# A chunk's triangular inverse, multiplied into b and into the output matrix before the chain

## The chip, the cores and the metric

The kernel runs on one core of a Trainium2 chip, in one launch. The metric is device time in microseconds, the median of several runs. The engines are named as in the profile: PE (TensorE, matmuls into PSUM banks), DVE (VectorE), ACT (ScalarE), POOL (GpSimd) and SP (SyncE, which issues every DMA). Work between engines is ordered by semaphores; each engine takes its own instructions in order.

## The reference: what is computed

One layer of a hybrid decoder, for a prompt of 1024 tokens and for 8 sample sequences of one token each, width 1024, all in fp32. A projection of 1024 x 9360 feeds two branches, a gated linear attention (GLA, 4 heads) and RWKV-7 (16 heads of 64); each branch is projected up, gated, merged, projected out and normed. The change is in RWKV-7 on the prompt, whose recurrence is, per head and token:

```python
def step(S, inp):
    rt, wt, kt, vt, kkt, at = inp
    sa = jnp.einsum('bhvk,bhk->bhv', S, -kkt)
    S = S * wt[:, :, None, :] + sa[..., None] * (kkt * at)[:, :, None, :] + vt[..., None] * kt[:, :, None, :]
    y = jnp.einsum('bhvk,bhk->bhv', S, rt)
    return S, y
```

Over a chunk of 64 tokens this can be written with matrices. With a, z, b and k the rows of the chunk scaled by their decays, the vectors sa solve a unit lower triangular system, whose matrix is built from a and b; the state at the chunk's end is the decayed sum of the old state, b times sa and k times v; and the outputs are z times the old state plus an output matrix (built from z, b and k) times sa and v. The inverse of the triangular system is known before the state is.

## The kernel before

**Tiling.** The tokens are done in two passes of 512 (the first takes the 8 samples along). The projection runs row by row: 128 output columns against 512 tokens in 24 matmuls a bank (8 blocks of the depth, three products each of high and low halves), in the first pass in two parts of 256 and 264 columns, into the PSUM banks `proj`. These are the matmuls `proj<-xs,wpart` of the profile; they make up most of PE's time and fill the gaps of everything else. Two RWKV heads are one pair, so there are 8 pairs in each pass and 16 in all, and each pair has 8 chunks of 64 tokens.

**Order.** The kernel is written as streams (generators that yield one instruction at a time). A planner, `Order.run`, picks at each step the stream whose next instruction can start first by its own cost table, with a priority by kind (`PRIO`, `ON_PE`), and so fixes every engine's order at build time. All instructions are therefore recorded on one line, L217, and are told apart by tiles. Buffers are handed out by tag (`get`, `free`). PSUM has 2 banks `proj`, 4 `big`, 1 `pch` and 1 `pY`. An engine called `self.C` lets the planner choose ACT or DVE, `self.E` DVE or POOL.

**A pair** goes through five stages.

- `front` makes the scaled rows: a and z in `az`, b and k in `bk`. PE multiplies them (`big<-az,bk`), and DVE masks the products into `gg`: per chunk the system's matrix (k index 0) and the output matrix (k index 1), for both heads. The diagonal 32x32 blocks of all systems go through DRAM (`LD`) into a layout with one block per partition, and DVE solves them in 31 steps, each one multiply (`Xt<-X,wide`) and one add (`X<-X,Xt`). The inverted blocks go through DRAM (`XD`) into the buffer `XT`, and into `X2`. There are two buffers `XT` of 128 x 1024.
- `back` makes the off-diagonal block of each 64x64 inverse: four transposes on DVE put blocks from `XT` in `X1`; four products on 128*32 tiles (`big<-X,L`), one copy to `A`, four products (`big<-X,A`), four copies into `XT`.
- `turn` transposes b and k (`big<-cons,bk`, the result `bt` again in the buffer `bk`) and v (into `u`, a buffer `wide`).
- `chain` goes through the chunks one after the other. Each has three products of 128x128 in the bank `pch`: the right-hand side (`pch<-wide,gg`), copied by DVE to a buffer `rh`; the inverse times it (`pch<-rh,XT`), copied as two 64x64 halves into `u` by ACT or DVE; and the state (`pch<-wide,bk`), from which DVE makes the next chunk's state. A chain starts when the chain of the pair before it has ended. At its end up to 16 products of 64x64 (z times the states, `pY<-row,az` and `big<-row,az`) and 16 of 128x64 (the output matrix times `u`, `pY<-wide,gg` and `big<-wide,gg`) make the outputs of the pair.
- `norm` norms and gates the outputs and stores them.

Each fp32 product stands in the trace as two matmul records.

Of the kernel before, what the change touches and what calls it, by code (L numbers as in the profile page):

```python
# [20 lines left out]
P = 128  # L21
# [11 lines left out]
C = 64  # L33
# [15 lines left out]
    "Xt": ([P, P], 1), "L1": ([P, P], 1), "A": ([P, P], 1), "S": ([P, GDV], 2), "Sp": ([P, C], 2), "s0p": ([P, C], 2), "rh": ([P, P], 2),  # L49
# [373 lines left out]
class Kern(Order):  # L423
# [711 lines left out]
    def front(self, c, p, st, d):  # L1135
# [95 lines left out]
        XT = (yield from self.get("XT")).rearrange("p (c h t) -> p c h t", c=NCH, h=2)  # L1231
# [21 lines left out]
        d.AZ, d.BK, d.G, d.XT, d.v, d.bonus, d.pc, d.L, d.L1, d.X2 = AZ, BK, GG, XT, st[2], st[1], pc, L_, L1, X2  # L1253

    def back(self, d):
        GG, XT = d.G, d.XT

        H = NCH // 2
        X1 = (yield from self.get("X1")).rearrange("p (x t) -> p x t", t=P)
        q = [slice(32 * n, 32 * n + 32) for n in range(4)]  # L1260
        for h in range(2):
            for n in range(2):
                g = 2 * h + n
                yield self.V.transpose(X1[q[g], :, q[g]], XT[q[2 * h], H * n:H * n + H, h, 0:32])
        pA = yield from self.bank("big", [P, P])
# [574 lines left out]
```

## Time and profile before

| | |
|---|---|
| median of 3 runs | 1489.15 us (1487.49, 1489.15, 1490.96) |
| profiled execution, its own time | 1487.92 us |
| its span, first to last instruction | 1486.1 us |
| busy PE, DVE, ACT, POOL | 1449.8, 1194.8, 857.7, 113.6 us |
| mean granted clock of PE | 0.996 |
| DMA | 318.96 MB, 66.8% of the 16 engines' span on the main queue |

A line of the groups reads: line, engine, operation, output tile <- input tiles, the array's rows*columns (PE), shape, count, then busy us and mean ns of one, then the engine's idle time just before them and what ended it. The timeline has start, duration, engine and count of merged neighbours. A line of a tile's view has the shortest, median and longest duration in ns and the first and last start in us.

### The profile page before, as it was taken

What the parts mean: (1) busy time and instruction counts of PE and PEld (TensorE: products, weight loads), DVE (VectorE), ACT (ScalarE), POOL (GpSimd) and SP (SyncE); (2) the same over time, 40 slices, a digit from 0 to 9 for tenths busy, and PEclk for the clock granted to TensorE, in tenths of its full rate; (3) what the DMA queues carried; (4) which work ended last, traced back from release to release, by engine and by line L of the source; (5) the groups of instructions that cost most, each with busy time, mean ns of one, the idle gap of its engine ahead of it and who ended that gap; (6) DMA issues with size and microseconds to landing.
All of it is one profiled execution on the core that took longest, in us unless ns stands there. A gap on an engine that the chain in (4) does not pass through costs nothing. (4 is left out here: it accounts for less than half of the span.)

```text
span 1486.1 us, 31563 instructions
## 1 busy us (share of the span) xinstructions
PE 1449.8 (98%) x11158; PEld 1260.4 (85%) x11158; DVE 1194.8 (80%) x3255; ACT 857.7 (58%) x2196; POOL 113.6 (8%) x208
## 2 busy tenths in 40 slices
PE   9999999999999999999999999999999999999997
PEld 6998999899989998787777777878787898988786
DVE  6697889888998899879878989898877866755665
ACT  5666776676767776665754555474547645544210
POOL 1001010201010102000101020111001000000000
PEclk9999999999999999999999999999999999999999
DMA  8886786678676877566566556656564766888432
GB/s 299 273 285 202 250 296 214 226 253 295 202 258 211 294 229 258 170 224 188 160 198 179 155 190 191 192 154 188 174 189 138 229 210 221 295 293 271 139 107 85
DMA packets 211258, 318.96 MB, mean 215 GB/s; under 512 B 91811, under 2 KB 107180, under 8 KB 211100
## 3 DMA queue, kind: packets, MB, share of 16 engines
q1 hardware_dynamic: 211100, 316.93, 66.8%
q8 instruction: 89, 1.46, 0.4%
q14 instruction: 69, 0.57, 0.1%
HBM read 197.19 MB, written 118.61 MB: 212 GB/s over the span
## 5 line engine op out<-in xcount | busy, mean ns | idle before, releaser
L217 PE MATMUL proj<-xs,wpart 128*128 128x264 f32 (+2 forms) x5640 | 1017.7, 327 | 1.4 <-DVE row L217 0.8
L217 PEld LDWEIGHTS proj<-xs,wpart 128*128 128x128 f32 x5640 | 808.5, 189 | 80.3 <-issue 9.9
L217 ACT CAST wpart<-wraw 128x512 fp32r<-128x512 f32 x210 | 130.2, 623 | 103.5 <-PE proj L217 49.6
L217 DVE TENSOR_TENSOR row<-row 128x512 f32<-128x512 f32 (+7 forms) x321 | 166.3, 524 | 12.4 <-ACT row L217 5.6
L217 DVE TENSOR_TENSOR wpart<-wraw,wpart 128x512 fp32r<-128x512 f32 x207 | 145.2, 702 | 32.3 <-ACT wpart L217 31.4
L217 ACT ACTIVATE row<-row 128x512 f32<-128x512 f32 (+5 forms) x213 | 128.8, 610 | 14.4 <-DMA row<-sg 6.5
L217 POOL TENSOR_TENSOR row<-row 128x512 f32<-128x512 f32 (+5 forms) x64 | 72.7, 1143 | 746.3 <-DVE row L217 396.4
L217 DVE TENSOR_TENSOR Xt<-X,wide 128x60 f32<-128x60 f32 (+24 forms) x496 | 104.8, 211 | 11.7 <-DMA wide<-LD 1.8
L217 DVE TENSOR_TENSOR X<-X,Xt 128x60 f32<-128x60 f32 (+24 forms) x496 | 105.4, 213 | 10.0
L217 ACT ACTIVATE row<-proj,omu 128x256 f32<-128x256 f32 (+1 forms) x99 | 54.0, 546 | 93.5 <-PE proj L217 93.3
L217 PE MATMUL big<-xs,wpart 128*128 128x256 f32 (+2 forms) x576 | 101.7, 332 | 0.0
L217 PEld LDWEIGHTS big<-xs,wpart 128*128 128x128 f32 x576 | 87.7, 194 | 9.7 <-issue 0.2
L217 DVE SCALAR_TENSOR_TENSOR wide<-pch,pc,s0p 64x64 f32<-64x64 f32 x208 | 58.7, 282 | 32.9 <-PE pch L217 28.0
L217 ACT COPY row<-wide 64x64 f32<-64x64 f32 x240 | 57.9, 241 | 40.2 <-DVE wide L217 34.7
L401 ACT ACT_TABLE_LOAD x62 | 79.5, 1283 | 1.1
L217 DVE SCALAR_TENSOR_TENSOR row<-proj,pv,row 128x255 f32<-128x255 f32 (+1 forms) x99 | 56.3, 569 | 22.4 <-ACT tail L217 13.7
L217 PE MATMUL big<-row 128*32 128x32 f32 (+4 forms) x936 | 65.3, 241 | 1.4 <-ACT row L217 1.4
L217 ACT COPY row<-big 128x128 f32<-128x128 f32 (+6 forms) x134 | 38.7, 318 | 42.2 <-PE big L217 36.7
L217 ACT COPY wide<-pch 64x64 f32<-64x64 f32 x159 | 32.8, 206 | 47.0 <-PE pch L217 45.1
L217 ACT ACTIVATE row<-proj 128x128 f32<-128x128 f32 (+4 forms) x136 | 36.9, 324 | 37.4 <-PE proj L217 37.0
L217 PE MATMUL pch<-wide,gg 128*128 128x128 f32 x256 | 51.6, 283 | 5.5 <-DVE wide L217 4.7
L217 PEld LDWEIGHTS pch<-wide,gg 128*128 128x128 f32 x256 | 42.3, 189 | 16.1 <-PE proj L217 4.7
(249 smaller groups left out, 1992.6 us busy)
## 6 DMA issues: line engine op xcount, KB each, us to landing
w<-wpart SPq DMA_DIRECT2D x146, 512.0 KB
wpart<-w SPq DMA_DIRECT2D x146, 512.0 KB
wraw<-w_in SPq DMA_DIRECT2D x146, 256.0 KB
wide<-LD SPq DMA_DIRECT2D x64, 128.0 KB
wraw<-w_up_gla SPq DMA_DIRECT2D x32, 256.0 KB
wraw<-w_up_rwkv SPq DMA_DIRECT2D x32, 256.0 KB
sg<-row SPq DMA_DIRECT2D x16, 260.0 KB
row<-sg SPq DMA_DIRECT2D x16, 260.0 KB
```

The lines of the kernel that those rows point to most:

```text
L217: ways.append((eng, lambda call=call: call(out, *args, **kw), price(eng, name, out, args, ins)))
L401: self.nc.scalar.preload_act_table_set(self.table)
```

## The change

The system is now solved the other way round: DVE goes through the columns from the last to the first, so that `X` becomes the inverse itself and not its transpose. Each step's multiply reads a column of `L` (`LT`, a view with 32 elements between neighbours) where it read a row; the 31 steps have the same sizes in the opposite order. The inverse of a chunk is kept per head without the zeros between the heads, as `XI`, in half of an `XT` buffer.

In `back`, `X1` is loaded from DRAM and `X2` is computed: the four products `big<-X,L` come first, four copies write `X2`, eight transposes of 32x64 write `A`, and the four products `big<-X,A` and four copies follow as before.

`turn` gets a new last step. For each chunk, each head and each of b (`bt`) and the output matrix (`gg`, k index 1), a 64x64 product with `XI`: 32 products, in two `big` banks, and eight copies of 64x256 which put the results back in place of b and of the output matrix.

In `chain` the product with `XT`, the copy to `rh` and the buffers `rh` are gone: the right-hand side itself is copied into `u`, as two 64x64 halves, and the state's product and the outputs use the multiplied b and output matrix.

The core of the diff:

```diff
@@ front
-        for j in range(31):
-            w, ni = 31 - j, j // 4 + 1
-            tv = tm[:, :ni * w].rearrange("p (s t) -> p s t", t=w)
-            yield V.tensor_mul(tv, X[:, 0:ni, j:j + 1].to_broadcast([P, ni, w]),
-                               L[:, j:j + 1, j + 1:].to_broadcast([P, ni, w]))
-            yield V.tensor_add(X[:, 0:ni, j + 1:], X[:, 0:ni, j + 1:], tv)
+        LT = L.rearrange("p s t -> p t s")
+        for j in range(31, 0, -1):
+            i, ni = j // 4, 8 - j // 4
+            tv = tm[:, :ni * j].rearrange("p (s t) -> p s t", t=j)
+            yield V.tensor_mul(tv, X[:, i:, j:j + 1].to_broadcast([P, ni, j]),
+                               LT[:, j:j + 1, :j].to_broadcast([P, ni, j]))
+            yield V.tensor_add(X[:, i:, :j], X[:, i:, :j], tv)
...
-        X2 = (yield from self.get("X2")).rearrange("p (g t) -> p g t", t=P)
+        X1 = (yield from self.get("X1")).rearrange("p (x t) -> p x t", t=P)
...
+        for h in range(2):
+            for n in range(2):
+                b, o = slice(64 * h + 32 * n, 64 * h + 32 * n + 32), h * NCH + H * n
+                yield self.S.dma_start(X1[b, :, b], XD[o:o + H].rearrange("c s t -> s c t"))
...
-                yield self.S.dma_start(XT[HS[h]][b, :, h, b], XD[n * NCH:(n + 1) * NCH].rearrange("c s t -> s c t"))
-
-        for x in range(H):
-            b = slice(32 * x, 32 * x + 32)
-            yield self.S.dma_start(X2[b, :, b], XD[2 * NCH + x::H].rearrange("g s t -> s g t"))
+                yield self.S.dma_start(XI[HS[h]][b, :, b], XD[n * NCH:(n + 1) * NCH].rearrange("c s t -> s c t"))
@@ back
-                yield self.V.transpose(X1[q[g], :, q[g]], XT[q[2 * h], H * n:H * n + H, h, 0:32])
...
-        yield self.C.copy(A_, pA)
+        for x in range(H):
+            for h in range(2):
+                yield self.V.transpose(A_[q[x], 2 * h:2 * h + 2], XI[q[2 * h + 1], x::H, 32:64])
+        for x in range(H):
+            yield self.C.copy(X2[q[x], :, x], pA[q[x]].rearrange("p (g t) -> p g t", t=32))
...
-                yield self.C.copy(XT[q[2 * h], H * n:H * n + H, h, 32:64], pZ[q[2 * h + n]])
+                yield self.C.copy(XI[q[2 * h + 1], H * n:H * n + H, 0:32], pZ[q[2 * h + n]])
@@ turn
+        pf = yield from self.get("big", 2)
+        pf = [y.rearrange("p (x k t) -> p x k t", k=2, t=C) for y in pf]
+        yield together([self.P.matmul(pf[h][HS[x % 2], x // 2, k], d.XI[hs, x], (bt[hs, x, h], d.G[hs, x, 1, h])[k], start=True, stop=True)
+                        for i in range(0, NCH, 2) for k in range(2) for x in (i, i + 1) for h, hs in enumerate(HS)], 0.5)
+        for k in range(2):
+            for h, hs in enumerate(HS):
+                for n in range(2):
+                    yield self.C.copy(d.G[hs, n::2, 1, h] if k else bt[hs, n::2, h], pf[h][HS[n], :, k])
+        self.free(*pf, d.XI)
@@ chain
             yield self.P.matmul(pr, GG[:, x, 0], u, start=True, stop=True)
-            rh = yield from self.get("rh")
-            yield V.tensor_copy(rh, pr)
-            self.free(pr)
...
-            pu = yield from self.bank("pch", [P, 2, C])
-            yield self.P.matmul(pu, XT[:, x], rh, start=True, stop=True)
-            self.free(rh)
             for h, hs in enumerate(HS):
-                yield self.C.copy(u[hs, h], pu[hs, h])
-            self.free(pu)
+                yield self.C.copy(u[hs, h], pr[hs, h])
+            self.free(pr)
```

The planner makes a new order of the whole program from it. PE, in the chain of the second pass's sixth pair, before (`proj` rows are projection matmuls, `big<-part,headsr` and `big<-az,bk` belong to the next pair's front):

```order
L217 MATMUL pch<-wide,gg 128x128
L217 MATMUL proj<-xs,wpart 128x512 x6
L217 MATMUL pch<-rh,XT_168 128x128
L217 MATMUL proj<-xs,wpart 128x512 x5
L217 MATMUL pch<-wide,bk 128x128
L217 MATMUL proj<-xs,wpart 128x512 x3
L217 MATMUL big<-part,headsr 128x512
L217 MATMUL proj<-xs,wpart 128x512
L217 MATMUL pch<-wide,gg 128x128
```

and the chunks of the same pair with the change:

```order
L217 MATMUL pch<-wide,bk 128x128
L217 MATMUL proj<-xs,wpart 128x512 x7
L217 MATMUL pch<-wide,gg 128x128
L217 MATMUL proj<-xs,wpart 128x512 x5
L217 MATMUL pch<-wide,bk 128x128
L217 MATMUL proj<-xs,wpart 128x512 x5
L217 MATMUL pch<-wide,gg 128x128
L217 MATMUL proj<-xs,wpart 128x512 x5
L217 MATMUL pch<-wide,bk 128x128
```

The middle product of a chunk is gone, and the projections between two products stay five to seven. Over the whole program the products `pch<-rh,XT` go from 128 to 0.

PE again, in the turn of that pair, with the change (before, only the transposes `big<-cons,bk` and `big<-cons,row` and 32 projections stood between the inverse and the chain):

```order
L217 MATMUL big<-X_173,A 32x128 x4
L217 MATMUL proj<-xs,wpart 128x512 x5
L217 MATMUL big<-cons,bk 128x64 x16
L217 MATMUL proj<-xs,wpart 128x512 x2
L217 MATMUL big<-cons,row 128x128 x4
L217 MATMUL proj<-xs,wpart 128x512 x5
L217 MATMUL big<-bk,XT_168 64x64 x4
L217 MATMUL big<-gg,XT_168 64x64 x4
L217 MATMUL big<-bk,XT_168 64x64 x4
L217 MATMUL big<-gg,XT_168 64x64 x4
```

The four groups of 64x64 products come twice (32 products, the last 16 follow), after everything that they read has been given some projections' time. Over the program the order has 512 of them.

DVE, in the same pair with the change, from the inverse to the first chunks of the chain:

```order
L217 STREAM_TRANSPOSE A<-XT_168 32x64 x8
L217 TENSOR_REDUCE row<-row 128x8
L217 BN_STATS st<-row 128x6
L217 BN_AGGR st<-st 128x2
L217 SCALAR_TENSOR_TENSOR row<-row,nkk 128x512
L217 COPY XT_168<-big 32x4x32 x4
```

Eight transposes stand where four of 32x128 stood. Of the 128 new copies of 64x256 over the program, the order has 49 on DVE and 79 on ACT; of the 256 copies of 64x64 in the chains, 159 on DVE and 97 on ACT, which were 97 and 159; of the 64 copies to `X2`, 5 on DVE and 59 on ACT, for 16 to `A`. DMA issues stay 1331.

More of the change, by code (lines that the diff above doesn't have):

```diff
@@ L1261, in back @@
         for h in range(2):
             for n in range(2):
-                g = 2 * h + n
-                yield self.V.transpose(X1[q[g], :, q[g]], XT[q[2 * h], H * n:H * n + H, h, 0:32])
-        pA = yield from self.bank("big", [P, P])
-        yield together([self.P.matmul(pA[q[x]], d.L1[:, x], X1[:, x], start=True, stop=True) for x in range(H)])
-        A_ = yield from self.get("A")
-        yield self.C.copy(A_, pA)
-        self.free(pA, X1, d.L1)
-        pZ = yield from self.bank("big", [P, H, 32])
@@ L1271, in back @@
-        yield together([self.P.matmul(pZ[q[g]], A_[:, q[g]], d.X2[:, g], start=True, stop=True) for g in range(4)])
-        for h in range(2):
-            for n in range(2):
-                yield self.C.copy(XT[q[2 * h], H * n:H * n + H, h, 32:64], pZ[q[2 * h + n]])
+                yield self.C.copy(XI[q[2 * h + 1], H * n:H * n + H, 0:32], pZ[q[2 * h + n]])
         for h, hs in enumerate(HS):
             yield self.C.copy(GG[hs, :, 0, h], d.AZ[hs, :, 0])
-        self.free(pZ, A_, d.X2)
+        self.free(pZ, A_, X2)
@@ L1353, in chain @@
         self.free(*pY, ss_)
-        self.free(AZ, BK, u_, GG, XT, pc)
+        self.free(AZ, BK, u_, GG, pc)
         if c.i:
```

24 lines of the change are left out of this document (15 added, 9 removed).

## The prediction

> **What bounds the kernel now.** The page first: the engines' busy shares and the slices of the span.
>
> ```profile
> span 1486.1 us, 31563 instructions
> ...
> PE 1449.8 (98%) x11158; PEld 1260.4 (85%) x11158; DVE 1194.8 (80%) x3255; ACT 857.7 (58%) x2196; POOL 113.6 (8%) x208
> ...
> PE   9999999999999999999999999999999999999997
> ...
> PEclk9999999999999999999999999999999999999999
> ```
>
> TensorE (PE) has work in every slice, at the full granted clock, and lacks only 36.3 us of the span (1486.1 - 1449.8). But matmuls overlap, so a row's busy time is no price: what one product costs the stream has to be read from start to start in the timeline. Before that, the groups of PE that the change touches (busy us, mean ns of one record, idle before it and who ended it):
>
> ```profile
> L217 PE MATMUL pch<-rh,XT 128*128 128x128 f32 x256 | 51.1, 281 | 4.1 <-DVE rh L217 4.1
> L217 PE MATMUL pch<-wide,bk 128*128 128x128 f32 x256 | 50.5, 279 | 2.0 <-DVE wide L217 1.3 <-ACT wide L217 0.7
> L217 PE MATMUL big<-X,A 128*32 128x128 f32 x128 | 7.0, 284 | 2.9 <-DVE row L217 1.3 <-DMA X<-XD 1.2 <-DVE A L217 0.3
> L217 PE MATMUL big<-X,L 128*32 128x128 f32 x128 | 6.8, 285 | 1.7 <-DVE X L217 1.7
> ```
>
> The first is the product that goes. An fp32 product stands as two records, so its 256 records are 128 products, eight in each of 16 pairs. Next, the timeline of a chain, PE alone (start, us, form, count):
>
> ```profile
> 139.76 1.33 PE L217 MATMUL proj<-xs,wpart 128*128 128x256 f32 x9
> 140.93 0.38 PE L217 MATMUL pch<-rh,XT 128*128 128x128 f32 x2
> 141.07 1.35 PE L217 MATMUL proj<-xs,wpart 128*128 128x264 f32 x9
> 142.25 0.38 PE L217 MATMUL pch<-wide,bk 128*128 128x128 f32 x2
> 142.39 1.45 PE L217 MATMUL proj<-xs,wpart 128*128 128x264 f32 x10
> 143.69 0.38 PE L217 MATMUL pch<-wide,gg 128*128 128x128 f32 x2
> 143.82 0.36 PE L217 MATMUL proj<-xs,wpart 128*128 128x256 f32 x1
> ```
>
> The chain's latency is not the bound. Between two of its products PE does 9 or 10 projection matmuls, and the last product of this kind starts long before the end of the span:
>
> ```profile
> L217 PE MATMUL pch<-rh,XT x256: 270/273/421, 136.7 to 1260.4; 128*128 128x128 f32 x128
> ```
>
> So a shorter chain gives nothing by itself. What counts is PE's own work, and PE's waits.
>
> **What leaves PE.** The chain of waits shows projections with nothing between them, 48 of 256 or 264 columns and 48 of 512:
>
> ```profile
> 1187.40 5.79 PE proj L217 x48
> ...
> 1315.04 11.11 PE proj L217 x48
> ```
>
> One takes 0.1206 us, or 0.2315 us. From 139.76 to 143.82 are 4.06 us with 28 projections (28 x 0.1206 = 3.38) and three products: (4.06 - 3.38)/3 = 0.228 us for each, half of the busy time that its group shows. 128 products leave: **-29.2 us**.
>
> **What comes to PE.** Per pair, 32 products of 64x64 by 64 columns, four different quadrants of the array in turn: 64 records, 512 products in all. The trace has the same form in the same order of quadrants, in the outputs' state part (16 products, 32 records):
>
> ```profile
> 894.24 0.95 PE L217 MATMUL proj<-xs,wpart 128*128 128x512 f32 x3
> 895.11 0.27 PE L217 MATMUL pY<-row,az 64*64 64x64 f32 x1
> ...
> 895.22 0.22 PE L217 MATMUL pY<-row,az 64*64 64x64 f32 x1
> ...
> 895.57 0.22 PE L217 MATMUL pY<-row,az 64*64 64x64 f32 x1
> ...
> 895.59 0.22 PE L217 MATMUL big<-row,az 64*64 64x64 f32 x1
> 895.74 0.69 PE L217 MATMUL pY<-wide,gg 128*64 128x64 f32 x16
> 896.25 0.64 PE L217 MATMUL big<-wide,gg 128*64 128x64 f32 x16
> 896.82 0.96 PE L217 MATMUL proj<-xs,wpart 128*128 128x512 f32 x3
> ```
>
> From 895.22 to 895.57 six groups of four records start, 0.058 us a group. The 32 records with the way out of the form take 895.11 to 895.74, 0.63 us; 32 more are eight groups, 0.46 us: 1.09 us. Going in, three projections and the change of form took 0.87 us where three take 0.69: up to 0.18 us. Coming back to projections, the second 16 records took 0.57 us against 0.51 for the first: 0.06 us. So a pair pays 1.09 to 1.33 us. I take 1.29 (the full entry may hold a little of what stands ahead of it): 16 x 1.29 = **+20.6 us**, ends 17.4 and 21.3. The products on 128*32 tiles keep their number.
>
> The Trainium skill says in "TensorE: Matmul & The Clock Gate", section "Wait — 56ns, not 53.3ns?", that start to start never drops below about 25 ns however small a matmul is; by that, an estimate, the 64 records would take 1.6 us and the 16 pairs some 29 us, and the change would give nothing on PE. The rows speak against it here: 0.058 us for four is 14.5 ns.
>
> **Waits.** The copy to rh goes with its 4.1 us of idle PE: -4.1. The product with bk now stands behind two copies of 64x64, as before, but the order puts 159 of these 256 on DVE instead of 97, and DVE is the engine that was late; it may inherit from nothing to the whole 4.1: I take +2, the middle, since its row shows 2.0 now with the smaller DVE share. The new block waits for the inverse (copies out of the big banks), and the first chunk for eight more copies; behind the block on PE stand projections, so all of PE waits with it, and its two big banks are held from the other streams till the copies are done. The nearest rows are the X products: (2.9 + 1.7) us on 32 blocks, 0.14 us a block; 16 new ones: +2.3, from 0 (the order puts projections and transposes ahead of them) to 16 x 0.53 us at which the whole gain is gone, a rival below.
>
> **What DVE and ACT get.**
>
> ```profile
> L217 DVE COPY rh<-pch 128x128 f32<-128x128 f32 x128 | 37.0, 289 | 17.5 <-PE pch L217 14.7
> L217 DVE COPY wide<-pch 64x64 f32<-64x64 f32 x97 | 21.4, 221 | 13.7 <-PE pch L217 11.3 <-issue 0.3
> L217 DVE STREAM_TRANSPOSE X<-XT 32x128 f32<-32x128 f32 x64 | 19.2, 300 | 4.9 <-DMA XT<-XD 4.3
> L217 DVE COPY wide<-big 64x256 f32<-64x256 f32 x31 | 13.1, 423 | 4.7 <-PE big L217 4.2
> ...
> L217 ACT COPY wide<-pch 64x64 f32<-64x64 f32 x159 | 32.8, 206 | 47.0 <-PE pch L217 45.1 <-DVE wide L217 0.3
> L217 ACT COPY wide<-big 64x256 f32<-64x256 f32 x33 | 12.1, 367 | 6.0 <-DVE wide L217 5.5
> L217 ACT COPY XT<-big 32x128 f32<-32x128 f32 x43 | 11.0, 256 | 7.3 <-PE big L217 6.7
> ```
>
> The order gives DVE 49 of the new 64x256 copies (49 x 0.423 = 20.7), 62 more chain copies (13.7) and 128 transposes of 32x64 for 64 of 32x128 (0.15 to 0.30 each; at 0.235 it is 30.1 - 19.2 = 10.9), and takes 128 rh copies (-37.0) and nine other 64x256 copies (-3.8): about +4.5 us. ACT gets 79 of the 64x256 copies (29.0) and 59 of 32x128 (15.1), less 62 chain copies (-12.8): about +31 us on an engine idle for 42% of the span. That cover hides both; without it, the eight copies at a hand-over (some 3 us on one engine) would keep projection banks full. The transfers stay as many and as large: four of 16 KB to X1 instead of four to X2, four of 32 KB to XI.
>
> The solve reads L down its columns, 128 bytes from element to element, in 31 multiplies a pair with 1560 elements in all. The trace has no long read of that kind. The nearest rows: the first product of a GLA head, whose writes jump (128x512, 128 elements apart), a plain 128x512, and two short ones, of which the last reads X with 128 bytes between its eight elements:
>
> ```profile
> 222.64 1.10 DVE L217 TENSOR_TENSOR row<-row 128x512 f32<-128x512 f32 x1
> ...
> 115.03 0.69 DVE L217 TENSOR_TENSOR row<-row 128x512 f32<-128x512 f32 x1
> ...
> 107.10 0.17 DVE L217 TENSOR_TENSOR Xt<-X,wide 128x16 f32<-128x16 f32 x1
> ...
> 108.51 0.16 DVE L217 TENSOR_TENSOR Xt<-X,wide 128x8 f32<-128x8 f32 x1
> ```
>
> The jumping write cost 0.41 us on 512 elements, 0.80 ns each; the jumping read of eight shows nothing. So 0 to 1560 x 0.80 ns = 1.25 us a pair on DVE; I take 0, by the row that also reads.
>
> **Sum**: -29.2 + 20.6 - 4.1 + 2.0 + 2.3 = -8.4 us. The profiled execution took 1487.92 us, its span and 1.8 us around it, so 1479.5. It lies 1.2 us under the median of the three runs, so the median should come to 1489.15 - 8.4, rounded **1481**.
>
> **Rivals.**
>
> *The gain comes back as waits* (no change, 1486 to 1492). The chain's three products a chunk become two, but both stand behind DVE. 256 products that wait 8.4/256 = 0.033 us longer eat it all; now rh and bk wait 6.1 us on 256 products, 0.024. For it: DVE at 80%, and a new order of everything. Against: DVE gets only 4.5 us more, and the order keeps five or more long projections between the chain's products. Chance 0.22.
>
> *The column read of L is slow and the inverse comes late* (slower). At 1.25 us a pair, unknown to the planner, PE stands at the X products and the new block; if every pair pays it, 16 x 1.25 = 20 us, 1481 + 20 = 1501. It is slower from (8.4 + 3)/16 = 0.71 us a pair. For it: the jumping write, and the 1.7 us that PE once waited for X. Against: the short read, and that the order has other work between solve and use. Chance 0.12. The Trainium skill speaks for this one: in "SBUF — State Buffer", section "Specifications (TRN2)", the row on cachelines says that full bandwidth needs two hits or more in a 16-byte line and that each step to a new line pays a penalty. The write agrees; no run here shows a long read.
>
> *The 64x64 block is dearer than its twin*, say as its 128x64 neighbours: 0.51 us for 16 records, 2.05 for 64, with 0.24 for the changes 2.29 us a pair, 36.6 us: -8.4 + 16.0 = +7.6, 1497. Against: same form, same order of quadrants, two banks in turn. Chance 0.09.
>
> That the change doesn't shorten the chain is out: the order shows two pch products a chunk.
>
> **How the numbers follow.** The forecast (PE's work falls) has 0.57. Its own range is 1470 (no new waits, the block at its low end, a few us by the new order) to 1486. The rivals have 0.22, 0.12 and 0.09. Range 1470 to 1496: it leaves out most of the late inverse and a little below. About 0.2%, 3 us, is what a measurement of this kernel can tell from no change. Faster by more 0.57; within it 0.24 (the second case and a mild form of the dear block); slower 0.19.
>
> **What the changed profile would show.** No rh group; pch products only with gg and bk; PE idle before the bk product near 4 us and not above 8. 512 products of 64x64 in 16 blocks of 1.2 to 1.4 us each: 2 us would be the dear block. Xt<-X,wide at the old duration for its size, for its largest form as here (with 0.80 ns on each of 76 elements it would be 305 ns):
>
> ```profile
> L217 DVE TENSOR_TENSOR Xt<-X,wide 128x76 f32<-128x76 f32 x16 | 3.9, 244 | 0.3
> ```
>
>  PE's busy time down by some 7 us, its idle time within 3 us of 36. I am wrong if PE's idle time grows by 8 or more, or if the new order leaves projections so late that the last chain's products start well after 1260.

## The result and the profile after

The changed kernel takes **1497.41 us** (median of 6 runs, 1493.07 to 1499.2); the kernel before took 1488.32 us beside it. The ratio is **1.0058, 95% interval 1.0038 to 1.0079**: slower by some 9 us, where 1481 was forecast, and above the range, which ended at 1496. The profiled execution took 1497.11 us, its span 1495.3. From the page of the changed kernel:

```profile
span 1495.3 us, 33318 instructions
PE 1445.9 (97%) x11926; PEld 1249.3 (84%) x11926; DVE 1210.3 (81%) x3249; ACT 882.2 (59%) x2283; POOL 136.1 (9%) x235
PE   9999999999989999999979999999999999999997
```

PE's busy time fell, 1449.8 to 1445.9, but its idle time grew from 36.3 to 49.4 us (1495.3 - 1445.9), 13.1 where the prediction had put its limit at 8. Two slices that were full are not full any more. The groups of the changed kernel by shape (busy us, mean ns | idle before, and what ended it):

```profile
L217 PE MATMUL pch<-wide,gg 128*128 128x128 f32 x256 | 51.7, 283 | 6.5 <-DVE wide L217 6.1 <-DMA wide<-Sp 0.2
L217 PE MATMUL pch<-wide,bk 128*128 128x128 f32 x256 | 51.7, 283 | 0.9 <-DVE wide L217 0.7
L217 DVE STREAM_TRANSPOSE A<-XT 32x64 f32<-32x64 f32 x128 | 30.3, 237 | 8.0 <-DMA XT<-XD 5.9
L217 PE MATMUL big<-part,headsr 128*128 128x512 f32 x64 | 27.6, 442 | 9.0 <-DVE Xt L217 7.7 <-DVE part L217 1.0 <-ACT bk L217 0.3
L217 PE MATMUL big<-bk,XT 64*64 64x64 f32 x512 | 16.8, 224 | 0.0
L217 PE MATMUL big<-gg,XT 64*64 64x64 f32 x512 | 16.0, 218 | 0.0
L217 PE MATMUL big<-X,A 128*32 128x128 f32 x128 | 7.1, 284 | 2.5 <-DVE A L217 1.4 <-ACT X L217 1.1
L217 PE MATMUL big<-X,L 128*32 128x128 f32 x128 | 6.8, 282 | 8.2 <-DMA XT<-XD 4.4 <-DMA X<-XD 2.4 <-DVE row L217 1.0
L217 DVE TENSOR_TENSOR Xt<-X,wide 128x76 f32<-128x76 f32 x16 | 4.7, 293 | 0.3
```

and two groups of the kernel before that the prediction does not show:

```profile
L217 PE MATMUL pch<-wide,gg 128*128 128x128 f32 x256 | 51.6, 283 | 5.5 <-DVE wide L217 4.7 <-ACT wide L217 0.3
...
L217 PE MATMUL big<-part,headsr 128*128 128x512 f32 x64 | 27.2, 430 | 3.8 <-DVE part L217 3.0 <-ACT part L217 0.7
```

The reader is to see three things. The chain's products wait less than before (6.5 + 0.9 us for 5.5 + 4.1 + 2.0), and the new block never waits. The first product of the inverse, `big<-X,L`, waits 8.2 us for 1.7, and 6.8 of the 8.2 ended with transfers out of `XD`; the second, `big<-X,A`, waits 2.5 us for 2.9. The multiplies of the solve take longer: 293 ns for the largest, 244 before.

The new block itself, in the timeline of PE in the changed kernel (start, us, form, count):

```profile
1078.87 1.40 PE L217 MATMUL proj<-xs,wpart 128*128 128x512 f32 x5
1080.21 0.34 PE L217 MATMUL big<-bk,XT 64*64 64x64 f32 x8
1080.37 0.30 PE L217 MATMUL big<-gg,XT 64*64 64x64 f32 x8
...
1081.07 0.30 PE L217 MATMUL big<-gg,XT 64*64 64x64 f32 x8
1081.30 1.19 PE L217 MATMUL proj<-xs,wpart 128*128 128x512 f32 x4
```

Five projections before it are 5 x 0.2315 = 1.16 us, to 1080.03; the next projections start at 1081.30. The block costs 1.27 us; 1.29 was forecast.

The longest wait of the changed kernel stands in the slice that shows 7. Its timeline, the rows that matter for it:

```profile
762.63 5.26 PE L217 MATMUL proj<-xs,wpart 128*128 128x512 f32 x22
...
763.69 2.33 POOL L217 TENSOR_TENSOR row<-row 128x512 f32<-128x512 f32 x1 [9.21 <-ACT row L217]
...
774.97 0.43 DVE L217 CAST part<-row 128x512 fp32r<-128x512 f32 x1
...
775.54 1.43 PE L217 MATMUL big<-part,headsr 128*128 128x512 f32 x2 [7.66 <-DVE Xt L217]
```

and two stretches of it, with the busy time of each engine and the granted clock:

```profile
core 0: us, PE busy (x) PEld busy (x) DVE busy (x) ACT busy (x) POOL busy (x), PEclk, DMA share, GB/s
...
765.00:772.00 7.00, 2.89 (x13) 2.03 (x11) 6.79 (x25) 4.73 (x10) 1.03 (x1) 1.00 0.50 152
772.70:779.50 6.80, 3.96 (x20) 2.95 (x21) 6.11 (x19) 1.04 (x2) 0.62 (x1) 0.50 0.07 12
```

In the planner's order this product follows a run of projections, and its `part` is there only at 775.40. Until then DVE, 6.79 of 7.00 us busy, works through two things at once: the solve of one pair and the rows that `big<-part,headsr` of the next needs. (The view names the multiply `Xt`, whose end lay nearest.) From 772.67, still in the wait, to 779.50 PE is granted half its clock. So a wait is followed by a loss of its own. To count this, I call *work* PE's busy time less half of its busy time at the half clock, the start-up included, and *idle* its gaps over 0.1 us up to the end of its last matmul, with the 1.7 us ahead of the first. The kernel before has work 1442.3 and idle 28.0, the changed kernel 1437.5 and 41.2; busy at half the clock before the end are 6.3 and 13.8 us. At the start PE is busy for 8.8 and 2.9 us before the full clock is granted; in the kernel before, projections start 0.22 us apart until then and 0.12 us after it. How long this lasts differs from execution to execution (full clock comes at 4.6 to 10.9 us in the twenty traces), so its share is no effect of the change. The 9.2 us of longer span are: work -4.8, idle with the ends +13.1, half clock +3.7, start-up -2.9.

### The profile page after: what moved, and what is told of

Read it like the earlier page. It is cut to its first block, busy times and chain, and to the rows that moved or that the text cites. A ratio compares the mean times of both kernels' runs of the same rounds, so it can differ in the third digit from the quotient of the medians.

```text
span 1495.3 us, 33318 instructions
## 1 busy us (share of the span) xinstructions
PE 1445.9 (97%) x11926; PEld 1249.3 (84%) x11926; DVE 1210.3 (81%) x3249; ACT 882.2 (59%) x2283; POOL 136.1 (9%) x235
## 4 chain that ended last, share of the span: by engine, by line
PE 40%; DVE 15%; DMA 6%; issue 4%; SPq 4%; ACT 3%; POOL 0%; POOLq 0%; DVEq 0%; ACTq 0%
PE proj L217 18%; PE big L217 17%; DVE row L217 5%; SPq L217 4%; PE pY L217 3%; DVE Xt L217 2%; DVE X L217 2%; PE pch L217 2%; ACT row L217 2%; DVE wide L217 1%; DMA wide<-LD 1%; DMA row<-xT 1%; DVE pair L217 1%; DVE wpart L217 1%; DMA XT<-XD 1%
## 5 line engine op out<-in xcount | busy, mean ns | idle before, releaser
L217 PE MATMUL proj<-xs,wpart 128*128 128x256 f32 (+2 forms) x5640 | 1008.2, 327 | 1.5 <-DVE row L217 0.8
L217 DVE TENSOR_TENSOR row<-row 128x256 f32<-128x256 f32 (+8 forms) x313 | 164.1, 530 | 7.3 <-ACT row L217 2.4
L217 DVE TENSOR_TENSOR wpart<-wraw,wpart 128x512 fp32r<-128x512 f32 x202 | 140.5, 698 | 32.2 <-ACT wpart L217 29.7
L217 POOL TENSOR_TENSOR row<-row 128x256 f32<-128x256 f32 (+4 forms) x72 | 78.1, 1090 | 642.1 <-ACT row L217 263.2
L217 DVE TENSOR_TENSOR Xt<-X,wide 128x60 f32<-128x60 f32 (+24 forms) x496 | 125.3, 253 | 13.0 <-DMA wide<-LD 1.7
L217 PE MATMUL big<-xs,wpart 128*128 128x512 f32 (+2 forms) x552 | 95.7, 328 | 1.7 <-ACT xs L217 1.3
L217 PEld LDWEIGHTS big<-xs,wpart 128*128 128x128 f32 x552 | 82.4, 191 | 11.2 <-ACT xs L217 1.5
L217 ACT CAST xs<-row 128x520 fp32r<-128x520 f32 (+1 forms) x64 | 38.5, 623 | 32.6 <-PE pY L217 9.8
L217 PEld LDWEIGHTS pch<-wide,bk 128*128 128x128 f32 x256 | 42.8, 189 | 12.6 <-issue 3.4
```

Source lines behind the costliest of these rows:

```text
L217: ways.append((eng, lambda call=call: call(out, *args, **kw), price(eng, name, out, args, ins)))
```

## The experiments

All runs stand beside the kernel before, whose median was 1487 to 1489 us each time. Labels are given as names. A trace is one execution, up to 4.5 us from the median of its kernel.

### The column read

**e1_row_read** is the changed kernel with a row of L read instead of the column. What it reads is zeros, so the inverse is the identity; the planner sees the same sizes, and the order on every engine is that of the changed kernel. **e2_before_col** is the reverse, the kernel before with the column read.

```diff
# e1_row_read, in the changed kernel
-                               LT[:, j:j + 1, :j].to_broadcast([P, ni, j]))
+                               L[:, j:j + 1, :j].to_broadcast([P, ni, j]))
# e2_before_col, in the kernel before
+        LT = L.rearrange("p s t -> p t s")
-                               L[:, j:j + 1, j + 1:].to_broadcast([P, ni, w]))
+                               LT[:, j:j + 1, j + 1:].to_broadcast([P, ni, w]))
```

> The changed kernel with one edit: each of the 31 multiplies of the solve reads a row of L where it read a column (it reads wrong numbers, so the inverse comes out as the identity). Every engine's order stays the same, instruction for instruction. Theory A (the column read costs 0.80 ns an element, 42 ns on the mean multiply, 20 us of DVE in all, and the late inverse and what DVE does behind it hold PE up): the multiplies fall from 253 to about 211 ns, the three PE waits of 7.7, 2.6 and 2.5 us go or shrink below 1 us, the clock has no more dips than before, and the time is that of the forecast, 1478 to 1484 us. Theory B (the waits come from the new order and from the new copies, and would stand with any multiply): 1494 us or more, with the long waits at the same places.

> The kernel before with one edit: the multiplies of its solve read a column of L where they read a row (wrong numbers, the inverse comes out as the identity), in the same order on every engine. Theory A: multiplies at 253 instead of 211 ns, 20 us more on DVE, and PE waits as in the changed kernel: 8 us or more, 1496 or later. Theory B: the old order has the slack for it, and the time stays within 3 us of 1488.

Measured: e1_row_read 1487.99 us (ratio to before 1.0008, 0.9993 to 1.0023), e2_before_col 1493.43 (1.0047, 1.0028 to 1.0065). The largest multiply, first in e1_row_read, then in e2_before_col:

```profile
L217 DVE TENSOR_TENSOR Xt<-X,wide 128x76 f32<-128x76 f32 x16 | 3.7, 234 | 0.3
```

```profile
L217 DVE TENSOR_TENSOR Xt<-X,wide 128x76 f32<-128x76 f32 x16 | 4.9, 307 | 0.3
```

Each order has its own pair: 234 ns with the row and 293 with the column in the order of the change, 244 and 307 in the order of before, 0.8 ns for each of 76 elements. All 496 multiplies of the changed order take 105.4 us with the row and 125.3 with the column, 1.25 us a pair. This is the upper bound of the prediction. In time it is worth 9.4 us in the changed order (1497.4 - 1488.0; 8.1 if each is counted against the kernel before that ran beside it) and 6.5 us in the order of before; a third pair of one order, below, gives 12.8. The wrong numbers are not what costs: the identity comes with the row in e1_row_read and with the column in e2_before_col, and the column is the slower in both. But with the row read the changed kernel is level with the one before, not at the 1478 to 1484 us of theory A, and its waits are still there. From e1_row_read:

```profile
L217 PE MATMUL big<-part,headsr 128*128 128x512 f32 x64 | 27.3, 433 | 8.7 <-DVE Xt L217 7.4 <-DVE part L217 1.3
L217 PE MATMUL big<-X,A 128*32 128x128 f32 x128 | 7.1, 284 | 1.3 <-DVE A L217 1.3
L217 PE MATMUL big<-X,L 128*32 128x128 f32 x128 | 6.8, 282 | 6.5 <-DMA XT<-XD 2.3 <-DMA X<-XD 1.8 <-ACT row L217 1.0
```

PE waits 7.4 us at the place of the 7.7, and 6.5 us for the first products. The slow read does not explain the missing 8 us of gain.

**e3_told** tells the planner of the slow read; **e4_act_copy** lets ScalarE write a transposed copy of L once a pair, so that DVE reads rows of it.

```diff
# e3_told, in the planner's price of a multiply
+        if name == "tensor_mul" and any(int(list(x.ap)[-1][0]) == 32 for x in ins):
+            return 0.068 + n / 960 + 0.0008 * n
# e4_act_copy
...
-        LT = L.rearrange("p s t -> p t s")
+        LT_ = yield from self.get("LT")
+        LT = LT_.rearrange("p (t s) -> p t s", s=32)
+        yield A.copy(LT, L.rearrange("p s t -> p t s"))
```

> The changed kernel, whose planner is told 0.8 ns an element more for the multiplies with the column read; the multiplies themselves stay slow. The planner makes another order. Theory A, if lateness against the plan is what costs: PE waits fall to the 28 us of before and the time to 1480 to 1487; if it is DVE's load itself that costs, 1490 to 1497. Theory B: any order may be lucky or not, 1485 to 1500, and the multiplies have no part in it.

> The changed kernel with L transposed once per pair by a copy on ACT (128 x 1024, some 1 to 2 us, on an engine 40% idle) into a buffer of its own, so that the multiplies read rows with the right numbers. Theory A: multiplies at 211 ns, time 1479 to 1486, a little above the run with the row read, since the copy stands in the pair's way for 1 to 2 us. Theory B: as the changed kernel, 1492 to 1500.

Measured: e3_told 1491.51 us (1.0031, 1.0015 to 1.0047), e4_act_copy 1507.33 (1.0139, 1.0117 to 1.0161). e3_told decides nothing: its time lies in the ranges of both theories, and PE's idle time, by the count above, is 36.3 us. e4_act_copy is slower than either of its theories allowed. The groups of e4_act_copy show why the copy is no cure:

```profile
L217 ACT COPY LT<-wide 128x1024 f32<-128x1024 f32 x16 | 33.4, 2086 | 3.2 <-DMA wide<-LD 3.1
...
L217 DVE TENSOR_TENSOR Xt<-X,LT 128x60 f32<-128x60 f32 (+24 forms) x496 | 107.6, 217 | 21.2 <-ACT LT L217 11.2
```

The multiplies are short again (217 ns in the mean), but the copy takes 2.09 us and stands ahead of the solve, where DVE sits idle for 11.2 us in all until it ends: more than the 1.25 us that it saves, on the path of every pair. The order is a new one too, so how much of the 10 us over the changed kernel is the copy's is open.

**e5_lay**, a complete kernel, stores X with the columns outer and the eight blocks inner, so that an element of L's column is read several times in a row; ScalarE brings the result back into rows.

```diff
-        X = X_.rearrange("p (i t) -> p i t", t=32)
+        X = X_.rearrange("p (t i) -> p t i", i=8)
...
+            tv = tm[:, :ni * j].rearrange("p (t s) -> p t s", s=ni)
+            yield V.tensor_mul(tv, X[:, j:j + 1, i:].to_broadcast([P, j, ni]),
+                               L[:, :j, j:j + 1].to_broadcast([P, j, ni]))
...
+        Y_ = yield from self.get("XY")
+        yield A.copy(Y_.rearrange("p (i t) -> p i t", t=32), X.rearrange("p t i -> p i t"))
```

> The changed kernel, complete, with the substitution's X stored columns outer and its 8 blocks innermost, so that L's column is read with each element repeated in the inner loop and not by a jump to the next; ScalarE copies X back into rows once per pair. Slow-read theory: the multiplies Xt go back from 253 ns to about 210 to 225 ns and the time falls to 1486 to 1491 us, near the row-read kernel's 1488.0. Rival (the order that comes out decides, whatever the read costs): the added copy shifts the order, and the time lies anywhere in 1470 to 1497 with the long PE waits deciding; the multiplies are short all the same.

Measured: 1494.04 us (1.0048, 1.0036 to 1.006). The multiplies are as short as expected, the time is 3 us above the range of the slow-read theory:

```profile
L217 ACT COPY XY<-X 128x256 f32<-128x256 f32 x16 | 11.3, 708 | 13.3 <-DVE X L217 13.2
...
L217 DVE TENSOR_TENSOR Xt<-X,wide 128x60 f32<-128x60 f32 (+24 forms) x496 | 110.5, 223 | 17.0 <-DMA wide<-LD 6.5
```

So a shorter solve alone is not enough. The copy adds 0.7 us to each pair's path, and the order is new; which of the two took the gain back is not separated here.

### Other orders of the same kernels

The planner fixes one order for each kernel. To see how much of a difference is the luck of that order, one of its numbers was changed slightly: `SPARE` (time it leaves for an operand of PE) from 0.4 to 0.42 (names with n1), or its hop price for products from 0.2 to 0.21 (n2).

```diff
# n1_before, n1_row, n1_after, e5_lay_n1
-SPARE = 0.4
+SPARE = 0.42
# n2_before, n2_row, e5_lay_n2
-HOP = {"P": 0.2, "D": 0.26, "G": 0.14, "V": 0.14, "A": 0.14}
+HOP = {"P": 0.21, "D": 0.26, "G": 0.14, "V": 0.14, "A": 0.14}
```

> The kernel before, with one constant of the planner moved by 0.02 us (SPARE 0.40 to 0.42, what it keeps free ahead of a PE instruction that waits for another engine): the same instructions in another order. Theory C (the old order was a lucky one; a new order of either program costs PE about 10 us in waits and clock): 1493 to 1502. Theory D (orders hardly differ, and the long waits come from what the change itself adds): within 4 us of 1487.

> The changed kernel with the row read (inverse wrong, as the identity) and SPARE 0.42: the changed instructions in another order, with fast multiplies. Theory C: the long waits of 7.4, 2.5 and 2.4 us are this order's own and lie elsewhere or not at all; time anywhere from 1478 to 1495, and on the mean of the orders some 8 us below the kernel before in the same two nudged orders. Theory D: waits of the same size at the same stages, 1486 to 1490.

> The kernel before, with another constant moved by 0.01 us (what the planner allows from PE to the engine that reads its bank, 0.20 to 0.21). Theory C: 1493 to 1502. Theory D: within 4 us of 1487.

> The changed kernel with the row read (inverse wrong, as the identity) and the second constant moved. Theory C: from 1478 to 1495, some 8 us below the kernel before with the same constant on the mean of the two. Theory D: 1486 to 1490, the 7 us wait of the headsr product at the start of the second pass stands again.

> The changed kernel, its column read kept, with SPARE 0.42. Slow-read theory: 1472 to 1477 us, 6 to 10 us above the row-read kernel at the same value (1466.3), since the column read cost 6.5 us in the order of before and 9.4 us in the changed order; TensorE's work, half-clock loss and waits taken apart, 7 us below that of the kernel before at this value. Rival (the slow read is hidden wherever no long wait lies): 1466 to 1469 us, as the row read.

> The same new layout with the planner's SPARE at 0.42 in place of 0.4, the value at which the row-read kernel took 1466.3 and the kernel before 1475.5. Slow-read theory with order as a second term: 1466 to 1476 us, below the kernel before at the same value. Rival (order alone): no relation to the other kernels at this value, 1470 to 1497 us.

> The same new layout with the planner's hop price for products at 0.21 in place of 0.2, where the row-read kernel took 1490.0 and the kernel before 1479.0. If the three nudges say anything of the layout itself, 1486 to 1491 us again; if order decides, anywhere in 1466 to 1497 us.

Measured, with the ratio to the kernel before: n1_before 1475.5 (0.9925, 0.9905 to 0.9946), n1_row 1466.29 (0.9867, 0.9848 to 0.9886), n2_before 1479.0 (0.9943, 0.9922 to 0.9964), n2_row 1490.03 (1.003, 1.0015 to 1.0044), n1_after 1479.08 (0.9946, 0.9931 to 0.9962), e5_lay_n1 1499.26 (1.0085, 1.0072 to 1.0098), e5_lay_n2 1491.76 (1.0028, 1.0016 to 1.004).

One and the same computation lies anywhere in a band of 11 us (before) to 24 us (row read), by nothing but the order, and with it the engine that takes an operation which may run on two. The theories missed this: n1_before and n2_before were to take 1493 to 1502 us or to stay within 4 us of 1487, and n1_row came 12 us below its lowest range. The order of the kernel before was the worst of its three, so a new order was no neutral thing. n1_row and n1_after have one order and differ in the read alone: 12.8 us. The expectation for n1_after was 1472 to 1477, and it came 2 us above; the rival, that the read is hidden (1466 to 1469), is out. That the new layout would follow the row read to 1466 to 1476 us with `SPARE` 0.42 was wrong by more than 20 us: a value of the planner's numbers doesn't carry its luck from one kernel to the next.

### The fold and the inverse apart

What was still open: which part makes the waits that the row read left. **fold_0** is the kernel before with the fold alone: the block, its copies and the chain of two products, but the inverse made in the old way (its transpose goes into the block, so the outputs are not the reference's). **inv_0** is e1_row_read without the fold: the new way to the inverse, and the old chain. The names with 1 and 2 have the planner's two values above.

```diff
# fold_0, in the kernel before: turn and chain as in the change, with
+        yield together([self.P.matmul(pf[h][HS[x % 2], x // 2, k], d.XT[hs, x, h], (bt[hs, x, h], d.G[hs, x, 1, h])[k], start=True, stop=True)
...
# inv_0, in e1_row_read: front and back as in the change, with
+        XT = (yield from self.get("XT")).rearrange("p (c h t) -> p c h t", c=NCH, h=2)
...
+            yield self.P.matmul(pu, XT[:, x], rh, start=True, stop=True)
```

> The kernel before with the fold alone: the 64x64 block and its 8 copies stand behind the turn, the chain takes two products, and the inverse is made as before (row read, X1 by transposes; its transpose goes into the block, so the numbers are wrong). TensorE's work should be about 7 us below before's 1442.8 in any case. Theory F (the fold itself, with its shorter chain, makes the waits): idle time between the first and the last matmul 33 us or more, with waits over 2 us, and 1484 to 1492 us. Theory I (the new making of the inverse makes them): idle 20 to 28 us, no wait over 2 us, 1474 to 1480 us. Theory C (each new order draws its own waits): neither holds at every value of the planner's numbers.

> The fold alone with SPARE 0.42, where the kernel before took 1475.5 us with 20 us of idle and the row-read changed kernel 1466.3 with as much. Theory F: idle over 28 us, 1476 us or more. Theory I: idle near 20 us, 1466 to 1470 us. Theory C: no relation.

> The fold alone with the hop price for products at 0.21, where the kernel before took 1479.0 us. Measured so far: the fold alone 1467.5 us in the first order and 1482.7 with SPARE 0.42, the inverse alone 1497.0 and 1484.4. Theory I (the new making of the inverse makes the waits): 1467 to 1477 us, below before at this value, with TensorE's work 7 us lower. Theory C (luck of each order): anywhere in 1465 to 1492 us.

> The changed kernel without the fold: the new making of the inverse (row read, X1 by transfers, A by transposes, so the inverse is the identity as in the row-read run), and before's chain with three products a chunk and the rh copy. TensorE's work as before, about 1443 us. Theory F: idle 20 to 28 us, no wait over 2 us, 1476 to 1487 us. Theory I: first products waiting for the transfers of XD 3 to 7 us in all and waits over 2 us, idle 33 us or more, 1488 to 1496 us. Theory C: neither at every value.

> The new making of the inverse without the fold, SPARE 0.42. Theory F: as the kernel before at this value, 1475 us with idle near 20 us. Theory I: 1480 us or more, with the waits for XD's transfers and a wait over 2 us. Theory C: no relation.

> The new making of the inverse without the fold, hop price 0.21. Theory I: slower than the kernel before at this value (1479.0), as in the other two orders (by 9 to 10 us): 1484 to 1496 us, with waits of the first products for XD's transfers. Theory C: anywhere in 1470 to 1497 us.

Measured: fold_0 1467.53 (0.9863, 0.9846 to 0.9879), fold_1 1482.73 (0.9974, 0.9962 to 0.9987), fold_2 1485.19 (0.9983, 0.9967 to 0.9999); inv_0 1496.98 (1.0068, 1.0053 to 1.0083), inv_1 1484.43 (0.9982, 0.9973 to 0.9992), inv_2 1483.67 (0.9966, 0.9951 to 0.998). All kinds in three orders (first, `SPARE` 0.42, hop 0.21); the last three columns are from the traces, in us: PE's work (mean), PE's waits for the transfers out of `XD`, and the time from the end of the solve to the second products `big<-X,A` (median over 16 pairs):

| kind | times | mean | work | idle | waits for XD | solve to second products |
|---|---|---|---|---|---|---|
| before | 1487.0, 1475.5, 1479.0 | 1480.5 | 1441.8 | 28.0, 20.0, 19.3 | 1.2, 0, 0.6 | 14.4, 14.6, 14.2 |
| fold alone | 1467.5, 1482.7, 1485.2 | 1478.5 | 1433.5 | 21.6, 31.3, 33.3 | 0.5, 0.2, 0 | 14.3, 14.6, 14.2 |
| inverse alone | 1497.0, 1484.4, 1483.7 | 1488.4 | 1441.7 | 32.6, 28.5, 26.1 | 5.7, 6.4, 7.7 | 17.4, 17.9, 17.1 |
| both, row read | 1488.0, 1466.3, 1490.0 | 1481.4 | 1434.2 | 33.2, 19.7, 35.6 | 4.1, 2.9, 5.1 | 17.2, 17.3, 17.0 |
| both, column read (the change) | 1497.4, 1479.1 | 1488.2 | 1437.4 | 41.2, 28.7 | 6.8, 4.0 | 17.2, 17.5 |
| both, X with columns outer (e5) | 1494.0, 1499.3, 1491.8 | 1495.0 | 1435.5 | 37.9, 45.2, 38.6 | 5.7, 19.3, 11.7 | 17.9, 18.8, 18.9 |

The columns say different things. *Work*: the fold takes 8.3 us out of PE (1439.9 to 1443.3 us in the three orders of before, 1433.1 to 1434.3 with it), and the inverse's new making nothing that shows (1438.5 to 1445.1). *Waits for XD* and *solve to second products* hang on the inverse alone, with no exception in twelve row-read orders: 0 to 1.2 us of waits and 14.2 to 14.6 us with the old making, 2.9 to 7.7 us and 17.0 to 17.9 with the new one. All waits of the two kinds of products `big<-X` together are 1.7 to 4.6 us with the old making and 5.1 to 12.1 with the new. What makes the path longer is seen in one pair. The kernel before, timeline:

```profile
905.25 0.18 DVE L217 TENSOR_TENSOR X<-X,Xt 128x8 f32<-128x8 f32 x1
905.49 2.58 SPq L217 DMA_DIRECT2D XD<-X  x4
911.43 1.85 SPq L217 DMA_DIRECT2D XT<-XD  x4
...
916.51 1.24 DVE L217 STREAM_TRANSPOSE X<-XT 32x128 f32<-32x128 f32 x4
...
918.17 0.43 PE L217 MATMUL big<-X,L 128*32 128x128 f32 x8
919.09 0.25 ACT L217 COPY A<-big 128x128 f32<-128x128 f32 x1
...
919.89 0.43 PE L217 MATMUL big<-X,A 128*32 128x128 f32 x8
```

and inv_0, the same pair:

```profile
905.16 0.17 DVE L217 TENSOR_TENSOR X<-X,Xt 128x8 f32<-128x8 f32 x1
905.39 2.57 SPq L217 DMA_DIRECT2D XD<-X  x4
911.32 1.79 SPq L217 DMA_DIRECT2D X<-XD  x4
913.15 1.91 SPq L217 DMA_DIRECT2D XT<-XD  x4
...
915.73 0.43 PE L217 MATMUL big<-X,L 128*32 128x128 f32 x8
919.28 1.99 DVE L217 STREAM_TRANSPOSE A<-XT 32x64 f32<-32x64 f32 x8
921.29 1.19 DVE L217 COPY X<-big 32x128 f32<-32x128 f32 x4
...
922.79 0.42 PE L217 MATMUL big<-X,A 128*32 128x128 f32 x8
```

In this pair of the kernel before, all that the second products need besides one copy of 0.25 us is there soon after the first products: 1.7 us from one to the other. With the new making the first products come 2.4 us earlier, with no transpose on DVE between the transfers and them; it is PE that waits for the transfers where they are late. But `A` needs the second four transfers and eight transposes of 0.24 us one after the other (1.99 us), which DVE begins 3.5 us after the first products, and `X2` four copies (1.19 us): 7.1 us from one to the other. Counted from the end of the solve, the second products stand at 17.5 us (905.33 to 922.79) where they stood at 14.5 (905.43 to 919.89). The first products' wait in the groups of fold_0, and of inv_0:

```profile
L217 PE MATMUL big<-X,L 128*32 128x128 f32 x128 | 6.8, 284 | 2.8 <-DVE X L217 1.4 <-issue 1.4
```

```profile
L217 PE MATMUL big<-X,A 128*32 128x128 f32 x128 | 7.0, 293 | 4.9 <-ACT X L217 4.9
L217 PE MATMUL big<-X,L 128*32 128x128 f32 x128 | 6.8, 282 | 7.2 <-DMA X<-XD 3.9 <-DMA XT<-XD 1.8 <-DVE row L217 1.0
```

In inv_0 PE waits 7.2 us before the first products, and once 4.9 us before the second, for the copy to `X2`. In the pair shown neither product waits: the projections of the order cover the longer path there.

*Time*: the inverse alone is slower than the kernel before in each of the three orders (by 10, 9 and 5 us). The fold alone is 20 us faster, 7 slower and 6 slower. With bands of 11 to 24 us, means of three orders differ by chance by several us, and a value of the planner's numbers pairs no orders, so the times settle less than the traces: the bands of the inverse alone and of before overlap (1483.7 to 1497.0 and 1475.5 to 1487.0 us). That the inverse's new making costs time is likely; its waits and its longer path are shown. The fold's 8 us of work are shown, and that they come out in the time is not. The fold's idle time was larger in two of the three orders; whether that is the fold's or the orders' is open. None of the three theories held throughout: theory I had the waits of the first products right at all three values, but fold_1 and fold_2 came 13 and 8 us above its ranges, and fold_0 lay below the ranges of both F and I.

Of the kernels that compute the whole, n1_before had the lowest median: the kernel before with `SPARE` 0.42, 1475.5 us, faster than before and after. The best order with the change complete, n1_after, took 1479.1, and the intervals of the two overlap.

## Why the prediction was wrong

**What bounds the kernel, what leaves PE and what comes**: right. No product with `rh` is left; the block cost 1.27 us for 1.29. With the change PE's work fell by 4.8 us in this pair of orders and by 2.7 with `SPARE` 0.42; in the means over three orders it fell by 7.6 us with the row read and by 8.3 with the fold alone, for 29.2 - 20.6 = 8.6. The sentence of the Trainium skill ("TensorE: Matmul & The Clock Gate", section "Wait — 56ns, not 53.3ns?") that start to start never drops below about 25 ns, by which 64 records would take an estimated 1.6 us, is not borne out here: from 1080.21 to 1081.07 seven groups of eight records start, 0.86 us, 15 ns a record, with four quadrants in turn.

**The column read, taken at 0**: wrong, and the step that failed beyond doubt. The prediction had the right bound, 1.25 us a pair, and then went by a read of eight elements, too short to show a slope (8 x 0.8 ns is 6 ns of 160). Measured: 1.25 us a pair on DVE, and 6.5, 9.4 and 12.8 us of time in three orders, each with its instructions in the same order and of the same sizes. In this order it is what takes the time from 1488.0, level with the kernel before, to 1497.4. The second rival had the mechanism right; its price of 20 us took every pair as exposed, and a third to two thirds of it came out in the time. The row on cachelines of the Trainium skill ("SBUF — State Buffer", section "Specifications (TRN2)") agrees: a step of 128 bytes goes to a new line at each element, and each costs 0.8 ns.

**The inverse's own path, not in the sum at all**: the second step that failed is "the products on 128*32 tiles keep their number" together with "the transfers stay as many and as large". Both are true, and neither is a price. Which transfer stands ahead of which product had changed: PE now waits directly for transfers, where DVE had waited for them, and `A` moved behind the second four. Measured: `big<-X,L` waits 8.2 us for 1.7 (6.5 with the row read), `big<-X,A` 2.5 for 2.9 (1.3), and the second products stand some 3 us further from the end of the solve in every order (17.0 to 17.9 us for 14.2 to 14.6).

What the row read left, 1488.0 where 1481 was forecast, comes apart in the traces of e1_row_read and before: work -6.0 us and start-up -2.9, against idle +5.2 and half clock +2.7. In the idle time the X products have +3.2, `big<-part,headsr` +4.9 and the chain's products -5.5; the rest is spread. The share of the X products belongs to the inverse's new making. Whether the wait at `headsr` is more than this order's luck is open: at the two other values the row-read kernel waits 1.2 and 6.5 us there, the kernel before 6.2 and 1.9.

**Waits in the chain and at the block**: better than forecast, but the chain's part by luck. The three groups of `pch` waited 11.6 us, the two wait 7.4: -4.2 for -4.1 + 2.0. In the two other orders of the kernel before the three groups wait only 5.0 and 5.9 us, and with the fold alone the two wait 4.4, 11.9 and 8.6: the fall was this order's (the `rh` product itself waits 2.0 and 2.8 us in the others), and over the orders none is shown. The block took no wait, for +2.3 with the first chunk. So the first rival's mechanism, 256 products that each wait a little longer, did not come. Its result (the gain comes back as waits) did, at the inverse and in three waits of 2.5 to 7.7 us ahead of which the order had no more projections.

**The new order, taken as neutral**: wrong in two ways. The order of before was 6 us worse than the mean of its three, so some gain was likely by luck alone; and a long wait is followed by half the clock, which was in no term (+3.7 us here). The range was set by the costs alone and should have held the order's share too: bands of 11 to 24 us were measured.

**What the changed profile would show**: the multiply at 293 ns was to be the sign of a slow read (305 was named), and the idle time's growth by 13.1 us passed the 8 at which the forecast was to be called wrong. Both signs pointed at the right places.

## What to carry to other kernels

When a change reroutes data, write down for each product which transfer, transpose or copy now comes last ahead of it, before and after: equal counts of instructions and transfers hide a path that is some 3 us longer. Price a strided read by a row long enough to show a slope, and where there is none, take the bound as its cost on the engine, not zero; how much of that reaches the time (here 6.5 to 12.8 of 20 us) is a question of its own. Where a planner sets the order, change one of its numbers slightly in both kernels and compare bands: here the bands of 11 to 24 us were wider than the 8 us under test.

## What the runs showed of the hardware

**A strided read on DVE** costs 0.8 ns an element more in fp32 at 128 bytes (234 to 293 and 244 to 307 ns for 76 elements). With the element repeated in the inner loop most of the price is gone (223 ns in the mean, against 253 with the column read and 212 with the row). On ACT the transposing copies took 2.09 us for 1024 elements and 0.71 us for 256.

**The granted clock falls after short waits.** Over all twenty traces, of 35 waits of PE of 2.0 us or longer 31 were followed by a stretch at half the granted clock, which began still in the wait or at most 1.6 us after PE's return; one of the other four lay inside such a stretch. Of 39 waits of 1.5 to 2.0 us 11 were followed by one that began by 3.5 us after the return, of 89 of 1.0 to 1.5 us 9. Of the 53 stretches five had no wait of 1.0 us ahead of them. They last 3.4, 6.8, 10.2 or 13.7 us. The Trainium skill ("TensorE: Matmul & The Clock Gate", section "HAM oscillation — how this bites in real kernels") warns of gaps above about 3.4 us; the stretches agree with windows of that length, but here waits of 2.0 us were mostly enough.

**A DVE operation can be held up by one of POOL.** Ahead of the long wait of the changed kernel an add of the solve took 1.25 us, where one of about its size in the same stretch took 0.22:

```profile
762.80 0.22 DVE L217 TENSOR_TENSOR X<-X,Xt 128x66 f32<-128x66 f32 x1
...
763.69 2.33 POOL L217 TENSOR_TENSOR row<-row 128x512 f32<-128x512 f32 x1 [9.21 <-ACT row L217]
...
764.85 1.25 DVE L217 TENSOR_TENSOR X<-X,Xt 128x60 f32<-128x60 f32 x1
```

It began while POOL worked on 128x512 elements and ended 0.08 us after POOL did. This is no single case. In the twenty traces 194 multiplies and adds of the solve took longer than 0.6 us; every one began while a two-input operation of POOL ran, and ended 0.02 to 0.16 us after it. The 19,466 that ran beside none took 0.31 us at most. Of all 285 that began inside one, 276 ended only after it. Beyond the median of their form these operations took 3.8 us in the kernel before and 6.9 in the changed kernel, 2.9 to 13.0 over all. No run took POOL's work away, so what this costs in time is not shown.
